# Paged decode attention inside a hybrid decoder layer: page order within a step, one list of cross-attention logit units, a tag for turned keys, and an earlier decay projection

## The chip, the cores and the metric

The kernel runs on one core of a Trainium2 chip (trn2). The metric is the device time of one execution in microseconds (us), lower is better. TensorE (PE in the profile) multiplies, VectorE (DVE), ScalarE (ACT) and GpSimd (POOL) work on vectors, SyncE (SP) issues nearly all DMA transfers, and each engine runs its own instructions strictly in the order in which they were written down for it.

## The reference, cut to what matters

One layer serves 512 prompt rows and 32 sample rows (8 sequences of 4 tokens) with the same weights; all arrays are float32.

```python
h = rmsnorm(x, norm_mix_g)
sq, sk, sv, gq, gk, gv, ga, gb, gz = split_cols(h @ w_in, IN_SPLITS)
o_sb  = stick_breaking_attention(q, k_all, v_all, ...)      # sample: 512 past tokens in 4 pages of 128, read through page_table
o_gdn = gated_delta_rule(...)                               # decay from ga, beta from gb
x = x + concat([o_sb, rmsnorm(o_gdn) * silu(gz)]) @ w_out
xq = rmsnorm((rmsnorm(x) @ w_xq).reshape(..., 4, 128))
attn = softmax(einsum('bshd,bmhd->bhsm', xq, mem_k) * 128 ** -0.5)   # sample: 256 cached memory tokens per sequence
x = x + einsum('bhsm,bmhd->bshd', attn, mem_v) @ w_xo
x = x + (silu(gate) * up) @ w_down
```

The change touches the sample side of the stick-breaking heads (`sb_sample`), the sample side of cross-attention (`cross_sample`), the decay of the gated-delta heads (`gates`), and the pacing of the gated-delta heads (`gdn_head`, `gdn_sample`, `invert`).

## The kernel before, in words

**Two kinds of work.** The dense work is projections: each float32 weight tile is split into a high and a low part (`wh`, `wl`) and each activation tile likewise (`ah`, `al`), and three products of 128x272 columns are accumulated for each half of the 544 rows (line 218; line 1598 for `w_xo`, line 2039 for gate and up, line 1919 for down). All else is side work, small matmuls with vector work between them: attention heads, the triangular inverses of the gated-delta heads, the sample rows.

**How the order is made.** Side work is written as Python generators. A `Side` object steps them from inside the dense loops (`side.tick` in `products`). Each `yield cost, latency` says how much PE time the step took and how long to leave that generator alone before its next step; the latency is counted in the dense and side time that was emitted meanwhile. A bigger latency puts more dense matmuls between a producer and its consumer. A scheduler then sets the final order of each engine's instructions. The feed-forward part (from about 1511 us on) is ordered by hand, and the change does not touch it.

**Stages.** Eight stick-breaking heads (to about 460 us), the decay columns (`gates`), eight gated-delta heads (to about 1050 us), the gates `gz`, `w_out` with the memory keys and values beside it, the `w_xq` projection, `w_xo` in two parts (columns 0 to 271, then 272 to 543; 16 blocks `m` of 12 matmuls each), then gate, up and down.

**`sb_sample`** runs twice, for heads 0 to 3 and 4 to 7. Its logits (`sample_logits`) go by units: a unit loads keys (`page`, 128x512), turns them with four transposes (line 968) into PSUM, ACT copies them to `kT` (line 699), and four matmuls at four column positions of the array multiply them with query windows `win` (line 711). Its values (`sample_values`) go by steps of four pages, one page for each of four sequences. Each page is one matmul of 128x512 at its own column position (line 752, `tile_position=(0, b * 32)`), so that four can run in the array at the same time. Six loads are kept ahead and seven buffers hold pages. A float32 matmul that is not a transpose is two instructions in the trace, so one page shows as x2 there and as x1 in the order.

**`cross_sample`** does the same for the 4 cross-attention heads: 16 units of keys (`xk`, line 1477), one pass over eight sequences for each of two pairs of heads, then a softmax (`xz`, `e`, from line 1487), then 16 value tiles (`xv`, line 1518), then a selection of the result (`selv`, line 1530). Its tiles come from the tags `ah` and `al` of the activation pool (16 buffers each) once the activations there are done: `c.tt` gives tag `ah`, `c.tp` gives tag `al`. It must be done before part 1 of `w_xo`: line 1585 drains the side work between the two parts.

```python
        if part:
            side.drain()
            pairs[-1].first()
```

**`gates`** (line 783) projects 16 columns of `w_in` for decay and beta, turns them, and makes the per-head factors; it is called once, after the eighth stick-breaking head was projected.

Of the kernel before, what the change touches and what calls it, by code (L numbers as in the profile page):

```python
# [15 lines left out]
P = 128  # L16
# [7 lines left out]
NB = 8  # L24
# [563 lines left out]
def sb_sample(c, g):  # L588
# [4 lines left out]
    for i, x in enumerate((q, k)):  # L593
        nc.vector.tensor_mul(sq[:, i * P : (i + 1) * P], x, x)
    yield 0.0, 2.0
    ps = c.aux()
# [34 lines left out]
    yield 0.3  # L631

    psz = c.aux()
    for h2 in range(2):

        def load(b, i):
            return load_pages(c, c.cache_k, [b * PAGES + i * 2 + j for j in range(2)], g * 4 + h2 * 2, 2)

        ps = yield from sample_logits(c, q, h2 * 2, load, 2)
        zt = c.tt("zt")  # L640
        nc.scalar.copy(zt[:, :256], ps[:, :256])
        yield 0.0, 1.0
# [32 lines left out]

def sample_logits(c, q, h0, load, n, ps=None, col=0):

    nc = c.nc
    w = c.tt("win")
    nc.gpsimd.memset(w[:, :512], 0.0)
    win = w[:, :512].rearrange("p (b h x) -> p b h x", b=NB, h=2)
    for b in range(NB):
        x = q[:, h0 * 32 : (h0 + 2) * 32].rearrange("p (h b t) -> p h b t", h=2, b=NB)[:, :, b]
        nc.gpsimd.tensor_copy(win[:, b, :, b * 4 : b * 4 + 4], x)
    yield 0.0, 3.0
    if ps is None:  # L690
        ps = c.aux()
    units = [(b, i) for b in range(NB) for i in range(n)]
    nxt = []

    def ahead():
        if units:
            pt = transposes(c, load(*units.pop(0)))
            k = c.tt("kT")
            nc.scalar.copy(k[:, :512], pt)
            nxt.append(k)  # L700

    ahead()
    yield 0.4, 0.2
    ahead()
    yield 0.4, 0.5
    for u in range(NB * n):
        b, i = divmod(u, n)
        k = nxt.pop(0)
        o = col + i * P
        for x in range(4):  # L710
            nc.tensor.matmul(
                ps[x * 32 : x * 32 + 32, o : o + P], win[:, b, x % 2, :], k[:, x * P : (x + 1) * P],
                start=u == 0 and col == 0, stop=b == NB - 1, skip_group_check=True, tile_position=(0, x * 32),
            )
        ahead()
        yield 0.7, 0.4
    return ps


def sample_values(c, w, n, load):  # L720
# [22 lines left out]
    for _ in range(6):  # L743
        ahead()
    yield 0.1, 1.5
    pso = c.aux()
    for half in range(2):
        ps = c.aux()
        for i in range(n):
            for b in range(4):  # L750
                x = ((i % 2) * NB + half * 4 + b) * 32
# [31 lines left out]
def gates(c, acts, rstd):  # L783
# [3 lines left out]
    ab = c.tt("ab")  # L787
    nc.vector.tensor_mul(halves(ab)[:16], ps[:16, :, :HT], halves(rstd)[:16])

    pt = c.aux()  # L790
# [109 lines left out]
def invert(c, gt, nc_, levels, res):  # L900
# [28 lines left out]
    for s in levels:  # L929
# [26 lines left out]
        nc.vector.tensor_sub(second[0], second[0], second[1])  # L956
        yield 0.22 * nc_, 1.1
        if s != levels[-1]:
# [80 lines left out]
def gdn_head(c, h, qkv):  # L1039
# [51 lines left out]
    for a in range(4):  # L1091
# [34 lines left out]
    nc.vector.tensor_mul(v3(on), v3(on), col(f, 4))  # L1126
    yield 0.0, 3.0
    ps = transposes(c, on)
# [16 lines left out]
def gdn_sample(c, g):  # L1145
# [294 lines left out]
def cross_sample(c, qs, outs, scale, tiles):  # L1440
# [13 lines left out]
    nc.vector.scalar_tensor_tensor(f, f, c.g_xq, r[:, :P], ALU.mult, ALU.mult)  # L1454
    yield 0.3, 2.5

# [10 lines left out]

    for h2 in range(2):
        if h2:
            some(0)  # L1470

        def load(b, i):
            if h2 or b >= 2:
                t = c.tt("xk")[:, :512]
            else:
                t = c.pb.tile([P, 4, P], F32, tag="wh", name="xk", bufs=XO_KEPT).rearrange("p k m -> p (k m)")
            nc.sync.dma_start(
                t.rearrange("p (a h d) -> p a h d", a=2, h=2), c.cache_mk[0, b, :, h2 * 2 : h2 * 2 + 2].rearrange("(a p) h d -> p a h d", p=P)
            )
            return t  # L1480

        ps = yield from sample_logits(c, f, h2 * 2, load, 1, ps if h2 else None, h2 * P)
    some(1)
# [753 lines left out]
def kern(ctx: ExitStack, tc: tile.TileContext, *args, stop=99):  # L2237
# [28 lines left out]
    with tc.tile_pool(name="pb", bufs=1) as pb:  # L2266
# [144 lines left out]
```

## Time and profile before

| what | us |
|---|---|
| median of 3 runs (2948.82 to 2950.75) | 2950.06 |
| the profiled execution | 2949.45 |
| its span, first to last instruction | 2947.8 |
| PE busy | 2864.5 |
| DVE busy | 2009.0 |
| ACT busy | 1447.9 |
| POOL busy | 721.7 |

The profile has a page for the whole execution and views for parts of it: sums in windows of time (with the granted TensorE clock, 1.00 being full speed, and the share of time that the 16 DMA engines were busy), a timeline of instructions with the idle time of the engine before each in brackets and what ended it, and a list of who waited for whom. Since matmuls are pipelined, a matmul's duration is not its cost: the cost is the distance from its start to the start of the next one.

### The profile page before, as it was taken

How to read it: one execution, taken by the hardware profiler on the slowest of the kernel's cores; microseconds unless marked ns; L12 is line 12 of the kernel's file. 1: busy time of each engine (PE TensorE's matmuls, PEld its weight loads, DVE VectorE, ACT ScalarE, POOL GpSimd, SP SyncE). 2: the span in 40 equal slices, each digit the busy share in tenths (PEclk: the TensorE clock that was granted, in tenths of full speed). 3: DMA queues.
4: the chain of work that ended last, by engine and by line, in shares of the span. 5: the costliest groups of instructions: out<-in, count | busy, mean ns of one | idle time of the engine just before them, and what ended most of it. 6: DMA issues, size and time to landing. Idle time of an engine off the chain costs nothing. (4 is left out here: it accounts for less than half of the span.)

```text
span 2947.8 us, 57119 instructions
## 1 busy us (share of the span) xinstructions
PE 2864.5 (97%) x22442; PEld 2725.5 (92%) x22442; DVE 2009.0 (68%) x3168; ACT 1447.9 (49%) x2760; POOL 721.7 (24%) x858
## 2 busy tenths in 40 slices
PE   8999999999999999999789999999999999999998
PEld 7997797788989999999679999999999999999998
DVE  5553344566686654437378888888888887888886
ACT  5455335443445354425555444444444446555675
POOL 3121111112212210003142343433333324211200
PEclk9999999999999999999899999999999999999999
DMA  7335534542343465532444554555455548966653
GB/s 224 94 95 151 173 97 132 166 125 70 97 132 86 119 214 152 151 114 83 151 140 120 169 169 150 162 161 161 149 163 169 150 135 259 272 199 199 189 172 96
DMA packets 632693, 442.72 MB, mean 150 GB/s; under 512 B 36107, under 2 KB 559704, under 8 KB 632424
## 3 DMA queue, kind: packets, MB, share of 16 engines
q1 hardware_dynamic: 600600, 384.64, 44.4%
q0 software_dynamic: 22176, 42.90, 4.7%
q10 hardware_dynamic: 9648, 11.54, 1.1%
q8 instruction: 176, 2.88, 0.4%
q14 instruction: 93, 0.76, 0.1%
HBM read 359.23 MB, written 79.75 MB: 149 GB/s over the span
## 5 line engine op out<-in xcount | busy, mean ns | idle before, releaser
L2039 PE MATMUL gu<-pr,wh 128*128 128x272 f32 x4944 | 674.4, 289 | 6.7 <-ACT pr L1668 3.0
L2039 PEld LDWEIGHTS gu<-pr,wh 128*128 128x128 f32 x4944 | 642.7, 189 | 8.4 <-ACT pr L1668 3.4
L218 PE MATMUL mm<-ah,wh 128*128 128x272 f32 (+1 forms) x2464 | 546.6, 301 | 6.0 <-ACT ah L334 3.7
L218 PE MATMUL mm<-al,wh 128*128 128x272 f32 (+1 forms) x2464 | 522.7, 291 | 0.7 <-DVE al L249 0.7
L218 PE MATMUL mm<-ah,wl 128*128 128x272 f32 (+1 forms) x2464 | 516.5, 290 | 0.1
L1919 PE MATMUL bank<-pr,wh 128*128 128x272 f32 x2464 | 466.6, 289 | 2.0 <-ACT bank L1947 1.3
L218 PEld LDWEIGHTS mm<-ah,wh 128*128 128x128 f32 (+1 forms) x2464 | 388.6, 188 | 37.9 <-issue 24.3
L207 DVE TENSOR_TENSOR wl<-wr,wh 128x512 fp32r<-128x512 f32 (+1 forms) x340 | 246.7, 729 | 233.0 <-ACT wh L206 227.0
L218 PEld LDWEIGHTS mm<-al,wh 128*128 128x128 f32 (+1 forms) x2464 | 388.8, 188 | 12.1 <-issue 9.1
L1919 PEld LDWEIGHTS bank<-pr,wh 128*128 128x128 f32 x2464 | 385.9, 188 | 4.1 <-ACT bank L1947 3.1
L218 PEld LDWEIGHTS mm<-ah,wl 128*128 128x128 f32 (+1 forms) x2464 | 386.1, 188 | 2.6 <-issue 1.0
L206 ACT CAST wh<-wr 128x512 fp32r<-128x512 f32 (+1 forms) x340 | 208.0, 614 | 325.4 <-PE mm L218 268.5
L2039 PE MATMUL gu<-pr,wl 128*128 128x272 f32 x2472 | 361.7, 289 | 2.0 <-DVE wl L1817 2.0
L1919 PE MATMUL bank<-pr,wl 128*128 128x272 f32 x1232 | 354.5, 288 | 0.0
L2039 PEld LDWEIGHTS gu<-pr,wl 128*128 128x128 f32 x2472 | 330.1, 189 | 2.4 <-issue 2.0
L1817 DVE TENSOR_TENSOR wl<-sum,wh 128x1024 fp32r<-128x1024 f32 x172 | 221.0, 1285 | 75.3 <-ACT wh L1813 75.3
L1919 PEld LDWEIGHTS bank<-pr,wl 128*128 128x128 f32 x1232 | 232.0, 188 | 0.0
L1813 ACT CAST wh<-sum 128x1024 fp32r<-128x1024 f32 x172 | 180.5, 1050 | 77.5 <-PE gu L2039 46.7
L1817 DVE TENSOR_TENSOR wl<-raw,wh 128x1024 fp32r<-128x1024 f32 x133 | 202.6, 1524 | 15.7 <-ACT wh L1813 13.7
L1813 ACT CAST wh<-raw 128x1024 fp32r<-128x1024 f32 x133 | 140.0, 1053 | 102.4 <-PE gu L2039 93.0
L2104 POOL DMA_DIRECT2D pr<-hT x154 | 82.1, 547 | 254.5 <-PE bank L1919 227.6
L1806 DVE TENSOR_TENSOR sum<-raw,sum 128x1024 f32<-128x1024 f32 x86 | 135.6, 1577 | 1.0
(530 smaller groups left out, 4173.2 us busy)
## 6 DMA issues: line engine op xcount, KB each, us to landing
raw<-in_w_gate_up SPq DMA_DIRECT2D x176, 512.0 KB
wr<-in_w_in SPq DMA_DIRECT2D x108, 512.0 KB
raw<-in_w_down SPq DMA_DIRECT2D x176, 256.0 KB
hT<-hs SPq DMA_DIRECT2D x154, 272.0 KB
pr<-hT POOLq DMA_DIRECT2D x154, 272.0 KB, 6.7
page<-in_cache_sb_k SPq DMA_DIRECT2D x128, 128.0 KB
page<-in_cache_sb_v SPq DMA_DIRECT2D x64, 256.0 KB
wr<-in_w_out SPq DMA_DIRECT2D x32, 512.0 KB
```

The source lines that it names most:

```text
L206: nc.scalar.copy(hi[:, :m, :n], raw[:, k : k + m, :n])
L207: nc.vector.tensor_sub(lo[:, :m, :n], raw[:, k : k + m, :n], hi[:, :m, :n].bitcast(F32))
L218: c.nc.tensor.matmul(ps[:n, h, :HT], l[:, :n], r[:, h * HT : (h + 1) * HT], start=first and i == 0, stop=last and i == 2,)
L1806: self.f.c.nc.vector.tensor_sub(self.a[q], self.a[x], self.a[y])
L1813: self.f.c.nc.scalar.copy(self.hi[q], self.left(q))
L1817: self.f.c.nc.vector.tensor_sub(self.lo[q], self.left(q), self.hi[q].bitcast(F32))
L1919: self.c.nc.tensor.matmul(self.c.bank[bank][:, o], t[x][:, s, i * P : (i + 1) * P], pairs[i].op[q][r], start=new and not (i or n), stop=se ...
L2039: self.c.nc.tensor.matmul(bank, w[:, i * P : (i + 1) * P], self.pairs[i].op[q][r], start=start and n == 0, stop=n == 23, skip_group_check= ...
L2104: self.c.nc.gpsimd.dma_start(t, self.hT[2 * g + pair, :, max(0, 2 * n - 1) + k])
```

## The change

Five edits, all in the order and pacing of the sample side work; no arithmetic is added or taken away.

1. **Values.** In a step of four pages, the matmul of the page that was loaded last (index 3) is emitted first, then 0, 1, 2, in `sample_values` and in `cross_sample`. The latency after a step of `sample_values` becomes 8.0 (from 1.0), after the first loads 5.0 (from 1.5), after a selection 3.0 (from 0.5).
2. **Logits.** `sample_logits` takes a list of units. The query windows are made ahead of it by `query_windows`, for both pairs of heads at once. In `cross_sample` all 16 units are one list, so the two-unit start of the pipeline occurs once instead of twice. The cost of a unit is stated as 0.6 (from 0.7).
3. **Turned keys.** `kT` comes from `c.tp`, seen as float32. In `cross_sample` this moves it from tag `ah` to tag `al`; in `sb_sample` both are the same tag.
4. **Decay.** `gates` becomes a generator: its projection is emitted ahead of the projections of the eighth stick-breaking head, the rest of it where it was.
5. **Latencies.** Larger ones in `sb_sample`, `invert`, `gdn_head` and `gdn_sample`.

```diff
@@ sb_sample
-    yield 0.0, 2.0
+    yield 0.0, 3.5
...
+    wins = [query_windows(c, q, h2 * 2) for h2 in range(2)]
+    yield 0.0, 5.0
     psz = c.aux()
     for h2 in range(2):
-        def load(b, i):
-            return load_pages(c, c.cache_k, [b * PAGES + i * 2 + j for j in range(2)], g * 4 + h2 * 2, 2)
-
-        ps = yield from sample_logits(c, q, h2 * 2, load, 2)
+        def load(b, i, h0=g * 4 + h2 * 2):
+            return lambda: load_pages(c, c.cache_k, [b * PAGES + i * 2 + j for j in range(2)], h0, 2)
+
+        ps = yield from sample_logits(c, [(wins[h2][b], i, load(b, i), b == NB - 1) for b in range(NB) for i in range(2)])
@@ 
-def sample_logits(c, q, h0, load, n, ps=None, col=0):
+def query_windows(c, q, h0):
     nc = c.nc
     w = c.tt("win")
...
-    yield 0.0, 3.0
-    if ps is None:
-        ps = c.aux()
-    units = [(b, i) for b in range(NB) for i in range(n)]
-    nxt = []
+    return [win[:, b] for b in range(NB)]
+
+
+def sample_logits(c, units):
+    nc = c.nc
+    ps = c.aux()
+    todo, nxt = list(units), []
 
     def ahead():
-        if units:
-            pt = transposes(c, load(*units.pop(0)))
-            k = c.tt("kT")
-            nc.scalar.copy(k[:, :512], pt)
+        if todo:
+            pt = transposes(c, todo.pop(0)[2]())
+            k = c.tp("kT")[:, :512].bitcast(F32)
+            nc.scalar.copy(k, pt)
             nxt.append(k)
...
-        yield 0.7, 0.4
+        yield 0.6, 0.4
@@ sample_values
-    yield 0.1, 1.5
+    yield 0.1, 5.0
...
-            for b in range(4):
+            for b in (3, 0, 1, 2):
...
-            yield 0.9, 1.0
+            yield 0.9, 8.0 if i < n - 1 else 1.0
...
-        yield 0.5, 0.5
+        yield 0.5, 3.0
@@ gates, behind the projection
     nc.vector.tensor_mul(halves(ab)[:16], ps[:16, :, :HT], halves(rstd)[:16])
+    yield
@@ invert, behind the second product of a level
-        yield 0.22 * nc_, 1.1
+        yield 0.22 * nc_, 1.7
@@ gdn_head
-        yield 0.22, 1
+        yield 0.22, 1.6
...
-    yield 0.0, 3.0
+    yield 0.0, 4.5
@@ gdn_sample, behind silu
-    yield 0.0, 4.0
+    yield 0.0, 6.5
@@ cross_sample
-    yield 0.3, 2.5
+    wins = [query_windows(c, f, h2 * 2) for h2 in range(2)]
+    yield 0.3, 5.0
...
-    for h2 in range(2):
-        if h2:
+    def load(b, h2):
+        if h2 == 1 and b == 0:
             some(0)
...
-        ps = yield from sample_logits(c, f, h2 * 2, load, 1, ps if h2 else None, h2 * P)
+    ps = yield from sample_logits(c, [(wins[h2][b], h2, lambda b=b, h2=h2: load(b, h2), b == NB - 1) for h2 in range(2) for b in range(NB)])
...
-            for b4 in range(4):
+            for b4 in (3, 0, 1, 2):
@@ kern
         for h in range(8):
             settle(h)
+            if h == 7:
+                decay = gates(c, acts, rstd)
+                next(decay)
...
-        gates(c, acts, rstd)
+        next(decay, None)
```

Three places of PE's order show what the edits move. In the rows, `page,win` is one page's value matmul, `kT,win` a unit's logit matmuls, `ident,xk` a unit's transposes, `mm` a dense projection.

Values of the first `sb_sample`, PE, before (a stretch of the second and third step):

```order
L752 MATMUL aux<-page,win 32x512
L218 MATMUL mm<-ah,wh 128x272 x2
L218 MATMUL mm<-al,wh 128x272 x2
L218 MATMUL mm<-ah,wl 128x272 x2
L752 MATMUL aux<-page,win 32x512
L218 MATMUL mm<-ah,wh 128x272 x2
L218 MATMUL mm<-al,wh 128x272 x2
L218 MATMUL mm<-ah,wl 128x272 x2
L752 MATMUL aux<-page,win 32x512 x2
```

The same place after the change:

```order
L218 MATMUL mm<-al,wh 128x272 x2
L218 MATMUL mm<-ah,wl 128x272 x2
L757 MATMUL aux<-page,win 32x512 x4
L218 MATMUL mm<-ah,wh 128x272 x2
L218 MATMUL mm<-al,wh 128x272 x2
L218 MATMUL mm<-ah,wl 128x272 x2
L533 MATMUL aux<-hat,raw 128x128
```

Before, a step's pages stand one or two at a time between dense matmuls; after, the four stand together. Over both calls of `sb_sample` the 64 value matmuls stand in 37 rows before (one of them holds seven, from the end of one step and the next) and in 20 rows after, 12 of four and 8 of two.

The end of the first part of `w_xo`, PE, before (the last row is the first of part 1):

```order
L968 MATMUL aux<-ident,xk 128x128 x4
L711 MATMUL aux<-kT,win 32x128 x4
L968 MATMUL aux<-ident,xk 128x128 x4
L711 MATMUL aux<-kT,win 32x128 x4
L1493 MATMUL aux<-xz,ident 64x128 x4
L968 MATMUL aux<-ident,e 128x128 x2
L1518 MATMUL aux<-xv,win 32x512 x8
L1530 MATMUL aux<-selv,os 128x16 x4
L1518 MATMUL aux<-xv,win 32x512 x8
L1530 MATMUL aux<-selv,os 128x16 x4
L1598 MATMUL mm<-xh,wh 128x272 x2
```

After the change, the value matmuls of cross-attention stand among the matmuls of part 0:

```order
L1523 MATMUL aux<-xv,win 32x512 x8
L1603 MATMUL mm<-xh,wh 128x272
L1603 MATMUL mm<-xl,wh 128x272
L1603 MATMUL mm<-xh,wl 128x272
L1603 MATMUL mm<-xh,wh 128x272
L1603 MATMUL mm<-xl,wh 128x272
L1603 MATMUL mm<-xh,wl 128x272
L1535 MATMUL aux<-selv,os 128x16 x4
L1523 MATMUL aux<-xv,win 32x512 x4
L1603 MATMUL mm<-xh,wh 128x272
L1603 MATMUL mm<-xl,wh 128x272
L1603 MATMUL mm<-xh,wl 128x272
```

Before, the last four units, the softmax and all values stand in one piece behind the last dense matmul of part 0; after, the last selection stands a block `m` ahead of the end of part 0, and no side work is left between the parts. On the way there, six units of `xk` and `kT` stand almost side by side, with one to three dense matmuls here and there.

The recurrence of a gated-delta head, PE, before (`ve,TT` makes what DVE scales into the operand of `ve,kn`):

```order
L1105 MATMUL aux<-ve,TT 128x128
L218 MATMUL mm<-ah,wl 128x272
L218 MATMUL mm<-ah,wh 128x272 x2
L218 MATMUL mm<-al,wh 128x272 x2
L218 MATMUL mm<-ah,wl 128x272 x2
L218 MATMUL mm<-ah,wh 128x272 x2
L1110 MATMUL aux<-ve,kn 128x128
```

The same step of the same head after:

```order
L1111 MATMUL aux<-ve,TT 128x128
L218 MATMUL mm<-ah,wh 128x272
L218 MATMUL mm<-al,wh 128x272 x2
L218 MATMUL mm<-ah,wl 128x272 x2
L218 MATMUL mm<-ah,wh 128x272 x2
L218 MATMUL mm<-al,wh 128x272 x2
L218 MATMUL mm<-ah,wl 128x272 x2
L218 MATMUL mm<-ah,wh 128x272 x2
L218 MATMUL mm<-al,wh 128x272 x2
L218 MATMUL mm<-ah,wl 128x272 x2
L1116 MATMUL aux<-ve,kn 128x128
```

Nine dense matmuls stood between the two, now seventeen. On SP, the first four of the loads of `xk` that wait for freed activation buffers stand ahead of the eighth load of `w_xo` instead of behind it, and the last five loads of `w_xo` stand behind the `xk` loads and most of the `xv` loads.

More of the change, by code (lines that the diff above doesn't have):

```diff
@@ L705, in sample_logits @@
     yield 0.4, 0.5
-    for u in range(NB * n):
-        b, i = divmod(u, n)
+    for u, (win, column, _, last) in enumerate(units):
         k = nxt.pop(0)
-        o = col + i * P
+        o = column * P
         for x in range(4):
             nc.tensor.matmul(
-                ps[x * 32 : x * 32 + 32, o : o + P], win[:, b, x % 2, :], k[:, x * P : (x + 1) * P],
-                start=u == 0 and col == 0, stop=b == NB - 1, skip_group_check=True, tile_position=(0, x * 32),
+                ps[x * 32 : x * 32 + 32, o : o + P], win[:, x % 2, :], k[:, x * P : (x + 1) * P],
+                start=u == 0, stop=last, skip_group_check=True, tile_position=(0, x * 32),
             )
         ahead()
-        yield 0.7, 0.4
+        yield 0.6, 0.4
     return ps
@@ L1466, in some @@
         values.append([loadv(i // 2 * 4 + b, i % 2) for b in range(4)])
-    for h2 in range(2):
-        if h2:
+    def load(b, h2):
+        if h2 == 1 and b == 0:
             some(0)
[L1472 to L1480, printed above, removed]
-        ps = yield from sample_logits(c, f, h2 * 2, load, 1, ps if h2 else None, h2 * P)
+        if h2 or b >= 2:
+            t = c.tt("xk")[:, :512]
+        else:
+            t = c.pb.tile([P, 4, P], F32, tag="wh", name="xk", bufs=XO_KEPT).rearrange("p k m -> p (k m)")
+        nc.sync.dma_start(
+            t.rearrange("p (a h d) -> p a h d", a=2, h=2), c.cache_mk[0, b, :, h2 * 2 : h2 * 2 + 2].rearrange("(a p) h d -> p a h d", p=P)
+        )
+        return t
+    ps = yield from sample_logits(c, [(wins[h2][b], h2, lambda b=b, h2=h2: load(b, h2), b == NB - 1) for h2 in range(2) for b in range(NB)])
     some(1)
```

## The prediction, as it was put on record before the changed kernel was run

> **What bounds the kernel now.** I read the page first, then the sums in windows, then TensorE's timeline in the two places where the windows differ from the rest, then the waits.
>
> ```profile
> PE 2864.5 (97%) x22442; PEld 2725.5 (92%) x22442; DVE 2009.0 (68%) x3168; ACT 1447.9 (49%) x2760; POOL 721.7 (24%) x858
> ...
> 1400.00:1500.00 100.00, 80.36 (x619) 63.93 (x618) 41.91 (x97) 52.37 (x130) 24.51 (x42) 0.86 0.45 140
> ...
> 1600.00:1700.00 100.00, 100.00 (x799) 100.00 (x798) 86.11 (x85) 46.31 (x61) 32.84 (x20) 1.00 0.52 156
> ```
>
> In the windows the columns are PE, weight load, DVE, ACT and POOL busy, the granted clock, the DMA share and GB/s. TensorE is the bound: it idles 2947.8 - 2864.5 = 83 us in all, and in a dense stretch it starts 799 matmuls in 100 us, 0.125 us each. So an edit here can gain in two ways only: it ends idle time of TensorE, or it shortens side work that takes TensorE from the dense matmuls. The stretch 1400 to 1500 stands out, with 619 matmuls and a clock of 0.86. It is cross-attention. Split at the end of part 0 of `w_xo` and at the start and end of part 1, and with TensorE's timeline from there, it shows why:
>
> ```profile
> 1404.00:1455.00 51.00, 45.19 (x373) 38.62 (x372) 25.32 (x58) 31.19 (x80) 11.45 (x28) 0.93 0.48 150
> 1455.00:1487.00 32.00, 18.18 (x114) 8.52 (x113) 5.35 (x17) 11.73 (x33) 4.87 (x7) 0.68 0.41 124
> 1487.00:1512.00 25.00, 24.90 (x194) 24.20 (x193) 21.65 (x45) 15.87 (x29) 13.01 (x10) 1.00 0.73 223
> ```
>
> ```profile
> 1455.30 0.28 PE L1598 MATMUL mm<-xh,wl 128*128 128x272 f32 x1
> 1457.12 0.63 PE L968 MATMUL aux<-ident,xk 128*128 128x128 f32 x4 [1.54 <-DMA xk<-in_cache_mem_k]
> 1458.58 0.63 PE L711 MATMUL aux<-kT,win 128*32 128x128 f32 x8 [0.82 <-ACT kT L699]
> 1461.18 1.08 PE L968 MATMUL aux<-ident,xk 128*128 128x128 f32 x4 [1.98 <-DMA xk<-in_cache_mem_k]
> ...
> 1473.13 0.66 PE L968 MATMUL aux<-ident,e 128*128 128x128 f32 x2 [2.13 <-DVE e L1396]
> 1475.45 3.64 PE L1518 MATMUL aux<-xv,win 128*32 128x512 f32 x16 [1.65 <-POOL acc L270]
> ...
> 1484.85 1.06 PE L1530 MATMUL aux<-selv,os 128*128 128x16 f32 x8 [0.68 <-ACT os L1526]
> 1486.61 0.52 PE L1598 MATMUL mm<-xh,wh 128*128 128x272 f32 x2 [0.70 <-ACT xh L1537]
> ```
>
> From 1455.4 to 1486.6 no dense matmul runs: four units, the softmax and the values go one after the other, each waiting for a load or another engine, at a clock of 0.68.
>
> **The values of `sb_sample`: 18 us.** In the timeline of the first call, x8 is four pages, x2 one, x4 two:
>
> ```profile
> 330.56 1.06 PE L752 MATMUL aux<-page,win 128*32 128x512 f32 x8 [0.40 <-POOL win L731]
> 331.56 0.52 PE L218 MATMUL mm<-ah,wh 128*128 128x272 f32 x2
> ...
> 334.59 1.04 PE L752 MATMUL aux<-page,win 128*32 128x512 f32 x2
> 335.56 0.52 PE L218 MATMUL mm<-ah,wh 128*128 128x272 f32 x2
> ...
> 336.52 1.05 PE L752 MATMUL aux<-page,win 128*32 128x512 f32 x4
> 337.50 0.52 PE L218 MATMUL mm<-ah,wh 128*128 128x272 f32 x2
> ```
>
> Start to next start, four pages take 331.56 - 330.56 = 1.00, one page 0.97, two 0.98. A group costs the same however many of the four column positions it fills. The order shows 37 rows of such matmuls before, of which the one with seven pages must be two groups, so 38, and 20 after. 18 x 0.98 = 17.6 us leave TensorE's path. The groups lie between dense matmuls with hardly an idle moment, so I take all of it: 18, from 14 (some groups still stretched by a late page) to 19.
>
> One rule speaks against so much. The Trainium skill ("TensorE: Matmul & The Clock Gate", Part 3, measured speedup) puts four packed row tiles at 3.07 times a single one, not four; by that estimate a full step would cost 0.98 x 4 / 3.07 = 1.28, the 12 full ones 12 x 0.3 = 3.6 more, and the gain would be 14. The row with x8 above, 1.00, says otherwise for columns, and the measurement decides.
>
> What the new order adds is a wait in front: the first matmul of a step now needs the last load, and behind it on TensorE stand the dense matmuls, that is everything. The loads keep six ahead of need, so a step's last two are issued when the step before it frees its pages:
>
> ```profile
> 331.64 16.03 SPq L777 DMA_DIRECT2D page<-in_cache_sb_v  x16
> ...
> PE aux L752 <- DMA page<-in_cache_sb_v: 0.2, 1, 0.2
> ```
>
> Before, 16 pages were issued in 16 us and TensorE waited for pages 0.2 us in all, so DMA gives a page per microsecond. The new latency of 8.0 sets the steps some 8 us of emitted work apart, four pages each. I cost the wait at nothing; the cover is that spacing, and without it the price is in the rivals.
>
> **Cross-attention: 16.5 us.** In the order after the change nothing stands between the parts, so the piece from 1455.42 to 1486.61, 31.2 us, goes, and its work moves among the matmuls of part 0. That work is not free. What a unit costs there is seen in the units that already lie there:
>
> ```profile
> 1443.16 0.29 PE L1598 MATMUL mm<-xh,wh 128*128 128x272 f32 x1
> 1443.29 0.60 PE L968 MATMUL aux<-ident,xk 128*128 128x128 f32 x4
> ...
> 1443.85 0.29 PE L1598 MATMUL mm<-xh,wl 128*128 128x272 f32 x1
> ...
> 1444.61 0.29 PE L1598 MATMUL mm<-xh,wl 128*128 128x272 f32 x1
> 1444.88 0.42 PE L711 MATMUL aux<-kT,win 128*32 128x128 f32 x8
> ...
> 1445.47 0.29 PE L1598 MATMUL mm<-xl,wh 128*128 128x272 f32 x1
> ```
>
> Two dense matmuls and the transposes take 1443.85 - 1443.16 = 0.69, so the transposes 0.44; likewise 0.86 - 0.25 = 0.61 for the logits. Four units are 4.2. `xz` is as narrow as a unit's logits, 0.6; the two transposes of `e` 0.2; 16 value matmuls in four groups at 0.98, 3.9; the selections at most their 1.06 each at the slow clock, say 1.8 together. Sum 10.7; 31.2 - 10.7 = 20.5 gained.
>
> Three things change that. First, in the 51 us of part 0 and the heads before it TensorE idles 5.8 already (51.00 - 45.19). Some of that goes, because `kT` no longer takes turns with `xk` in one tag and the first `xk` loads no longer queue behind a load of `w_xo` on SP: 3 gained (0 to 5.8). Second, six units now stand almost side by side, each `kT` needing ACT's copy of the unit just turned; the tail above shows 0.8 for that wait, so 4 lost (0 to 8, the upper end with a stretch of half clock). ACT on average has room: 31.19 + 11.73 = 43 us in the 62 that the stage would take. Third, the tail was a rest for DVE, 5.35 of 32.00, while in part 1 behind it DVE has 21.65 of 25.00. What it caught up there now falls into part 1 and the start of gate and up: 3 lost (0 to 6). The loads of `w_xo` that moved behind `xv` I cost at nothing: the cover is that six blocks of part 1 keep their weights, 6 x 12 x 0.125 = 9 us in which the next can land. Together 20.5 + 3 - 4 - 3 = 16.5, from 8 to 26.
>
> **The latencies and the decay: 8 us.** The waits of TensorE between 190 and 1060 us at whose producers a `yield` grew, or a step moved:
>
> ```profile
> PE aux L1110 <- DVE ve L1106: 4.7, 5, 2.8
> PE aux L913 <- DVE TT L956: 3.1, 3, 1.6
> PE aux L1166 <- POOL sqk L859: 2.7, 2, 1.5
> PE aux L968 <- DVE on L1126: 2.1, 3, 1.3
> PE aux L597 <- DVE sq L594: 2.0, 2, 1.0
> PE aux L792 <- DVE ab L788: 1.7, 1, 1.7
> PE aux L711 <- POOL win L688: 1.5, 1, 1.5
> ```
>
> They sum to 17.8. The order shows eight dense matmuls more, 1.0 us, between `ve,TT` and `ve,kn`, which covers most such waits but not the longest, 2.8, where DVE was late for its own reasons. Where one wait goes the next is somewhat late. I take a little under half, 8, from 0 to 18. The decay projection moves with its two narrow weight loads ahead of the eighth head's loads; the same matmuls run, and its wait of 1.7 is in the sum. The windows made at once are two memsets and 16 small copies on POOL, 24% busy, earlier by one pass; that is in the 1.5.
>
> A wait can also cost clock, and here trace and rule part:
>
> ```profile
> 766.00 2.74 PE L1206 MATMUL aux<-sqk,s 128*128 128x8 f32 x24
> ...
> 769.00:776.00 7.00, 7.00 (x36) 7.00 (x34) 0.54 (x2) 1.11 (x2) 1.02 (x1) 0.51 0.45 131
> ```
>
> Behind 24 matmuls of eight columns the clock is 0.51 for 7 us, with TensorE busy all the time. That costs up to 3.5 us, and the order after has a longer run of these, 20 matmuls or x40 in the trace, so I expect it again and count no gain. The Trainium skill (same page, "HAM oscillation") gives the rule as no idle gap over some 3.4 us; by it neither this stretch nor the tail, whose longest wait is 2.13, should have slowed, and the clock could neither give nor take here. The trace disagrees in both places; the sum stays 8, with 3.5 either way inside its bounds.
>
> **Sum.** 18 + 16.5 + 8 = 42.5. From the profiled execution, 2949.45 (1.65 outside its span, 0.6 below the median of the runs), this gives 2907.
>
> **The rivals.** *Cross-attention gives it back:* part 0 becomes a chain of copies and waits, and DVE's backlog lands on gate and up. For it: DVE's 21.65 of 25.00; against: ACT's 43 in 62. Then cross-attention brings 4 and the sum is 30: 2919. *Everything goes:* part 0 swallows all without a wait, and three quarters of the waits in the heads go: 19 + 26 + 14 = 59, 2890. *The last page blocks:* if each of the 16 steps waits for its last page, the whole core waits. The point from which it decides is (42.5 + 5.9) / 16 = 3.0 us a step; at 4 us the time is 2949.45 - 42.5 + 64 = 2971, slower. For it: four pages are 1 MB, and SP issues them in line with weight loads that may block; against: the 0.2 above. *It doesn't do what it says:* the groups close up, but TensorE then idles for weights as long, and the stage of cross-attention is held by its loads: within 6 us of 2949.
>
> **How the numbers follow.** Forecast 0.60 (its own range 2894 to 2917), given back 0.18, everything 0.15, last page 0.04, no change 0.03. The bound of what counts as a change is 0.2%, 5.9 us. The bounds of the terms add up to 22 (14 + 8 + 0) and 63 (19 + 26 + 18), which is 2927 and 2886; this range takes in the first three cases and leaves out the ends of the last two. Faster 0.93, same 0.03, slower 0.04.
>
> **What would show it.** Right: `page,win` in the timeline as x8 at about 1.00; no stretch without dense matmuls between the two parts of `w_xo`, part 1 starting some 45 us earlier than 1486.6 (18 from the values, 8 from the heads, 19.5 from part 0); the waits for `ve` and `TT` at about half. Wrong: a wait for `page` of microseconds before each step; `kT` or `xk` waits in part 0 summing to over 10 us; long waits for `pr` or `wl` at the start of gate and up; or the sum of the waits in the heads unchanged under new names.

## The result and the profile after

The changed kernel takes 2918.34 us (median of four runs, 2914.71 to 2921.17) where the kernel before takes 2949.44 beside it: a ratio of 0.9898, 95% interval 0.9880 to 0.9915, or 30 us less. The forecast was 2907, the range 2886 to 2927. The profiled execution is 2919.49, 30.0 below that of before, and it is read here. First the page's row of TensorE, after the change:

```profile
PE 2844.4 (97%) x22442; PEld 2726.1 (93%) x22442; DVE 2006.2 (69%) x3168; ACT 1447.2 (50%) x2760; POOL 718.9 (25%) x858
```

TensorE is busy for 20 us less with the same 22442 matmuls, so most of the gain is matmul time and not idle time. Where it lies is found by taking the same dense matmul in both traces, since their number and sequence are the same. The 5377th, at the end of the attention heads, starts at 1077.1 before and 1069.7 after: 7.4 gained. The first of part 1 of `w_xo` starts at 1486.6 and 1458.6: 28.0 gained. The end is 30.0 earlier. So what lies between the two, cross-attention above all, brought 20.6 and the heads 7.4, where the prediction had 16.5 and 26.

The timeline of TensorE in the first `sb_sample` after the change has the value matmuls as forecast:

```profile
326.83 1.07 PE L757 MATMUL aux<-page,win 128*32 128x512 f32 x8
327.83 0.52 PE L218 MATMUL mm<-ah,wh 128*128 128x272 f32 x2
...
337.22 1.07 PE L757 MATMUL aux<-page,win 128*32 128x512 f32 x8
338.21 0.52 PE L218 MATMUL mm<-ah,wh 128*128 128x272 f32 x2
```

Four pages stand together and take 1.00 and 0.99, start to next start, without a wait in front. The sums in windows for part 0 of `w_xo` with all of cross-attention, and for the start of part 1, and below them TensorE's timeline at the seam:

```profile
1396.00:1458.60 62.60, 56.15 (x485) 44.90 (x483) 29.72 (x72) 42.10 (x110) 15.59 (x34) 0.97 0.54 177
1458.60:1486.00 27.40, 27.26 (x196) 26.41 (x197) 22.79 (x48) 16.65 (x33) 13.99 (x12) 0.94 0.73 225
```

```profile
1444.06 1.92 PE L1523 MATMUL aux<-xv,win 128*32 128x512 f32 x16
...
1446.78 1.05 PE L1535 MATMUL aux<-selv,os 128*128 128x16 f32 x8
...
1447.75 1.07 PE L1523 MATMUL aux<-xv,win 128*32 128x512 f32 x8
...
1453.65 1.06 PE L1535 MATMUL aux<-selv,os 128*128 128x16 f32 x8
...
1458.60 0.52 PE L1603 MATMUL mm<-xh,wh 128*128 128x272 f32 x2 [2.29 <-ACT xh L1542]
```

The 31 us without dense matmuls are gone; what is left of the seam is one wait of 2.29. Part 0 is at a clock of 0.97, and ACT's 42.10 in 62.60 left room for the copies of `kT`.

The heads are where the forecast failed. The waits of TensorE between 190 and 1060 us after the change (total, times, longest):

```profile
PE aux L960 <- DVE X L956: 6.2, 2, 4.5
PE aux L715 <- POOL win L686: 4.1, 2, 2.8
PE aux L919 <- DVE TT L962: 3.9, 2, 3.3
PE aux L1111 <- DVE ve L1108: 3.1, 3, 1.3
PE aux L974 <- POOL cv L865: 2.3, 3, 1.0
PE aux L715 <- ACT kT L704: 1.8, 2, 1.3
```

These are the longest; all rows of this view add up to 30.5, against 24.3 before. The waits for `ab` (1.7) and for `ve` at `ve,kn` (4.7, now 1.1) went as forecast, and longer ones came for `X`, `win` and `TT` (`X` and `TT` are tiles of the triangular inverses).

To follow this through the experiments I split the time up to the 5377th dense matmul into three accounts. *Waits* is the idle time ahead of matmuls, counted above 0.1 us. *Clock* is half of the time in which TensorE was busy at half clock, an upper estimate: in the changed kernel two dense matmuls take 0.45 there, start to next start (754.87 to 755.32), and 0.25 at full clock. *Work* is the rest. The count starts at the first dense matmul, which is 0.3 earlier after the change, so that the heads show 7.1 here and not 7.4. Differences against the kernel before, in us, each from one profiled execution:

| kernel | work | waits | clock | heads in all |
|---|---|---|---|---|
| changed | -21.5 | +5.8 | +8.6 | -7.1 |
| values alone | -24.1 | +8.9 | +6.5 | -8.8 |
| latencies of the heads alone | -5.4 | 0.0 | -3.4 | -8.8 |
| changed, head latencies as before | -23.3 | +4.9 | -0.4 | -18.7 |
| changed, late convolution | -25.2 | +2.1 | +2.5 | -20.6 |
| changed, scalings on DVE | -20.5 | -0.7 | +3.4 | -17.8 |
| page order alone | -25.4 | +10.6 | +6.8 | -8.0 |
| pace of the values alone | -25.0 | +8.5 | +4.1 | -12.4 |
| changed, `kT` in its old tag | -21.9 | +5.7 | +11.9 | -4.3 |
| changed, two lists | -22.1 | +6.1 | +11.6 | -4.4 |
| head latencies as before, late convolution | -21.9 | -1.5 | -1.7 | -25.1 |
| head latencies as before, scalings on DVE | -23.2 | -3.3 | -2.0 | -28.6 |

The work fell by more than the 18 that the forecast gave it. Waits and clock took 14 of it back. The rows for `kT` in its old tag and for two lists show how far one execution is to be trusted: up to there both kernels have the same order on TensorE as the changed one, and their clock differs from its by 3.

### The profile page after: what moved, and what is told of

It is laid out like the page before. It is cut to its first block, busy times and chain, and to the rows that moved or that the text cites. A ratio compares the mean times of both kernels' runs of the same rounds, so it can differ in the third digit from the quotient of the medians.

```text
span 2917.8 us, 57065 instructions
## 1 busy us (share of the span) xinstructions
PE 2844.4 (97%) x22442; PEld 2726.1 (93%) x22442; DVE 2006.2 (69%) x3168; ACT 1447.2 (50%) x2760; POOL 718.9 (25%) x858
## 5 line engine op out<-in xcount | busy, mean ns | idle before, releaser
L218 PEld LDWEIGHTS mm<-ah,wh 128*128 128x128 f32 (+1 forms) x2464 | 389.7, 189 | 33.7 <-issue 20.5
L1822 DVE TENSOR_TENSOR wl<-raw,wh 128x1024 fp32r<-128x1024 f32 x133 | 202.9, 1527 | 15.3 <-ACT wh L1818 13.4
```

The lines of the kernel that those rows point to most:

```text
L218: c.nc.tensor.matmul(ps[:n, h, :HT], l[:, :n], r[:, h * HT : (h + 1) * HT], start=first and i == 0, stop=last and i == 2,)
L1822: self.f.c.nc.vector.tensor_sub(self.lo[q], self.left(q), self.hi[q].bitcast(F32))
```

## The experiments

Three theories were tried. *One:* the larger latencies cost by themselves, since waits move on to the next consumer. *Two:* the slower pace of the values pushes `sb_sample` and `gdn_sample` to other places beside the gated-delta heads, and that costs. *Three*, formed after the first four runs: POOL's convolution of the sample rows holds up one operation that DVE needs, and DVE, in order, holds up TensorE. Each kernel was timed against the kernel before on its own chip, and times are compared by these ratios: a ratio times 2949.44 stands for us.

**The parts alone.** First the values:

```diff
-    yield 0.1, 1.5
+    yield 0.1, 5.0
-            for b in range(4):
+            for b in (3, 0, 1, 2):
-            yield 0.9, 1.0
+            yield 0.9, 8.0 if i < n - 1 else 1.0
-        yield 0.5, 0.5
+        yield 0.5, 3.0
```

> The kernel before with the page order (3, 0, 1, 2) and the three latencies of the values alone. Both theories expect groups of four pages as x8 at 1.00 us and 17.5 us less of TensorE's time for the values. Theory one (the larger latencies of the heads cost by themselves, the values are innocent) expects nearly all of it as time: 2949.4 - 17.5 = 2932, from 2929 to 2936, and waits of the heads as before. Theory two (the slower pace of the values pushes them into the gated-delta heads, and that displacement costs) expects the loss of about 10 to be here: 2942, from 2938 to 2948, with more groups of the state update ex,kns and more half clock.

Ratio 0.9960 (0.9946 to 0.9973), 12 us less. Its waits between 560 and 1060 us begin so:

```profile
PE aux L954 <- DVE X L950: 7.3, 3, 4.6
PE aux L940 <- DVE X L936: 4.1, 1, 4.1
```

The page matmuls cost 20.4 less, but the waits for `X` of the changed kernel are here too, without any larger latency in the heads. That speaks for theory two. Then cross-attention, with the windows made ahead and the page order of its values:

```diff
-            k = c.tt("kT")
-            nc.scalar.copy(k[:, :512], pt)
+            k = c.tp("kT")[:, :512].bitcast(F32)
+            nc.scalar.copy(k, pt)
...
-    for h2 in range(2):
...
+    ps = yield from sample_logits(c, [(wins[h2][b], h2, lambda b=b, h2=h2: load(b, h2), b == NB - 1) for h2 in range(2) for b in range(NB)])
```

> The kernel before with the edits of cross-attention alone: one list of units, windows ahead, kT in the other tag, the page order of its values. Both theories expect what the stage gained in the full change, 20 us: 2929, from 2926 to 2933. If the stage gains only because the heads before it end otherwise, it is less than 12: over 2937.

Ratio 0.9907 (0.9891 to 0.9922), 27 us less, more than the 20 expected; by the profiled executions 22.9, of which 0.7 lie in the heads, where TensorE's order is that of the kernel before. Behind the heads it gains 22.2, the changed kernel 22.5, so this part does not depend on the others. Then the larger latencies:

```diff
-    yield 0.0, 2.0
+    yield 0.0, 3.5
...
-        yield 0.22 * nc_, 1.1
+        yield 0.22 * nc_, 1.7
...
-        yield 0.22, 1
+        yield 0.22, 1.6
...
-    yield 0.0, 3.0
+    yield 0.0, 4.5
...
-    yield 0.0, 4.0
+    yield 0.0, 6.5
```

> The kernel before with the five larger latencies of the heads alone (sb_sample 3.5, invert 1.7, gdn_head 1.6 and 4.5, gdn_sample 6.5), the decay where it was. Theory one expects slower by about 8: 2957, from 2952 to 2963, with ve,kn waits of TensorE down by about 3 and waits for TT up by more. Theory two expects the gain that the prediction gave them, 8 less: 2941, from 2936 to 2946.

Ratio 0.9975 (0.9962 to 0.9987), 7 us less: theory one falls in this form. But its waits between 190 and 1060 us show that the prediction's reason was wrong as well:

```profile
PE aux L1105 <- DVE ve L1102: 5.5, 6, 1.6
PE aux L940 <- DVE X L936: 4.0, 1, 4.0
```

All rows add up to 24.9, against 24.3 before. The wait of 2.8 at `ve,kn` is gone and others stand one consumer on. What fell is work, by 5.4, and the cost of half clock, by 3.4. Of the work about 3 is page groups that closed, 34 rows of `page,win` in place of 37, which the prediction's values term counts already. And the reverse, the changed kernel with four of the latencies as before:

```diff
-        yield 0.22 * nc_, 1.7
+        yield 0.22 * nc_, 1.1
...
-        yield 0.22, 1.6
+        yield 0.22, 1
...
-    yield 0.0, 4.5
+    yield 0.0, 3.0
...
-    yield 0.0, 6.5
+    yield 0.0, 4.0
```

> The changed kernel with the latencies of invert, gdn_head and gdn_sample as before (1.1, 1, 3.0, 4.0); page order, pace of the values, cross-attention, decay and the 3.5 of sb_sample as changed. Theory one expects the loss to go: 2918.3 - 9 = 2909, from 2905 to 2914. Theory two expects the small gain of the latencies to go and the loss to stay: 2924, from 2919 to 2928.

Ratio 0.9870 (0.9855 to 0.9885), 38 us less, so 8 better than the changed kernel (0.9898), though the ends of the two intervals overlap. The same latencies bring 7 alone and cost about 8 beside the other edits. Each result fits one theory, this one the first and the one before the second; neither foresaw both. The three parts alone bring 12 + 27 + 7 = 46 by the ratios, each with an interval of some 4 us either way, near the prediction's 42.5; together they bring 30. By the profiled executions it is 39 against 30. The rest of the change (the windows made at once in `sb_sample`, the stated cost of a unit there, the earlier decay) was run in no kernel by itself, so its share of the difference is not known.

**What the latencies do in company.** The account says clock: 15.4 us lost to half clock in the heads of the changed kernel, 6.4 with the old latencies, a difference three times the 3 us between executions of one order. Beside it `ex,kns`, the update of the sample states, costs 3.9 of work more than in the kernel before. TensorE's timeline of the changed kernel, and the sums over the stretch around it:

```profile
747.72 0.96 PE L1212 MATMUL aux<-sqk,s 128*128 128x8 f32 x8
748.53 1.14 PE L955 MATMUL aux<-T,gt 128*128 128x128 f32 x8
749.50 5.14 PE L1212 MATMUL aux<-sqk,s 128*128 128x8 f32 x40
```

```profile
743.70:760.10 16.40, 16.40 (x117) 16.30 (x116) 5.57 (x15) 5.72 (x13) 1.31 (x2) 0.79 0.34 100
```

With the old latencies the same matmuls stand in groups of eight records among dense matmuls:

```profile
749.22 0.95 PE L1212 MATMUL aux<-sqk,s 128*128 128x8 f32 x8
750.03 0.49 PE L218 MATMUL mm<-ah,wh 128*128 128x272 f32 x2
...
750.86 0.95 PE L1212 MATMUL aux<-sqk,s 128*128 128x8 f32 x8
```

```profile
741.00:761.00 20.00, 20.00 (x170) 19.50 (x168) 7.90 (x14) 5.40 (x10) 1.31 (x2) 1.00 0.60 173
```

TensorE is busy throughout both stretches; only the mixture differs, and the clock is 0.79 in the one and 1.00 in the other. The prediction knew of this longer run of narrow matmuls in the order and counted it at no change. The matmuls of `ex,kns`, each on 32 rows of the array, are written in pairs that run side by side:

```profile
804.15 1.99 PE L1265 MATMUL aux<-ex,kns 32*128 32x512 f32 x8
806.07 0.52 PE L218 MATMUL mm<-ah,wh 128*128 128x272 f32 x2
...
813.15 1.12 PE L1265 MATMUL aux<-ex,kns 32*128 32x512 f32 x2
814.20 0.52 PE L218 MATMUL mm<-ah,wh 128*128 128x272 f32 x2
```

Two pairs take 1.92, and one matmul that lost its partner takes 1.05, as much as a pair. The order has them in 7 rows before, 10 after, 7 again with the old latencies. It is what the change mended for the pages, undone for another group. That the order of these groups decides the clock is argued from the two stretches; no run changed it alone.

**Pace or page order.** The two halves of the values' edit, each alone on the kernel before:

```diff
-            for b in range(4):
+            for b in (3, 0, 1, 2):
```

> The kernel before with the page order (3, 0, 1, 2) alone, the latencies of the values as they were (1.5, 1.0, 0.5). In the order it has 16 rows of page,win, so the groups close without the latencies. If the slower pace of the values is what brings the extra waits and half clock of the values-alone kernel, this one keeps the whole 17 to 20 us: 2949.4 - 18 = 2931, waits of the heads near the 29 us of before. If any shift of the work brings them, it lands with the values-alone kernel, about 12 below the kernel before: 2938. And a step of four pages behind a short latency may now wait for its last page, at 1 us per page up to 2 us for each of 16 steps.

Ratio 0.9945 (0.9929 to 0.9961), 16 us less. The groups close (21.4 less for `page,win`), and the wait comes that the prediction had left to the pace; its first row of waits:

```profile
PE aux L752 <- DMA page<-in_cache_sb_v: 10.5, 12, 2.4
```

The other half:

```diff
-    yield 0.1, 1.5
+    yield 0.1, 5.0
-            yield 0.9, 1.0
+            yield 0.9, 8.0 if i < n - 1 else 1.0
-        yield 0.5, 0.5
+        yield 0.5, 3.0
```

> The kernel before with the three latencies of the values alone (5.0, 8.0, 3.0), pages in the old order. In the order it has 17 rows of page,win, as few as with the page order. If the pace is what closes the groups and what shifts the heads, it equals the values-alone kernel, about 12 below the kernel before: 2938. If the page order is needed as well, groups of one and two pages show in the timeline and the gain is under 6.

Ratio 0.9958 (0.9941 to 0.9974), 12 us less, and `page,win` 20.4 less. So the pace closes the groups by itself, the page order does so too, and neither adds to the other. The pace pays with waits for `X` (4.7 and 4.1 the longest), the order with waits for pages. So theory two holds for the waits for `X`, but not for the loss as a whole: the heads gain 8.0 with the order alone, without any slower pace, and 8.8 with both.

**What holds X.** In the changed kernel TensorE waits 4.54 for `X` at 708.73:

```profile
708.73 1.98 PE L960 MATMUL aux<-TT,X 128*128 128x128 f32 x8 [4.54 <-DVE X L956]
```

DVE's timeline ahead of it, and below it POOL's, where L1163 and L1165 are the convolution of the sample rows in `gdn_sample`:

```profile
699.91 0.90 DVE L1073 SCALAR_TENSOR_TENSOR cumrow<-cumrow,neg 128x512 f32<-128x512 f32 x1
706.27 0.69 DVE L1083 TENSOR_TENSOR gt<-gt,aux 128x512 f32<-128x512 f32 x1 [5.45 <-POOL gt L1082]
707.38 0.69 DVE L1088 TENSOR_TENSOR cumrow<-cumrow,aux 128x512 f32<-128x512 f32 x1 [0.43 <-POOL cumrow L1087]
707.99 0.68 DVE L956 TENSOR_TENSOR X<-aux,lev 128x512 f32<-128x512 f32 x1
```

```profile
695.55 0.42 POOL L1163 TENSOR_TENSOR sqk<-raws,convw 128x128 f32<-128x128 f32 x1
...
704.78 0.45 POOL L1165 TENSOR_TENSOR sqk<-sqk,sctmp 128x128 f32<-128x128 f32 x1
705.19 1.04 POOL L1082 TENSOR_TENSOR gt<-cumrow,sm 128x512 f32<-128x512 f32 x1
```

POOL works through the convolution from 695.55 to 705.19, with one other operation in between, and only then scales `gt`. DVE stands for 5.45 before it, and `X`, two places behind on DVE, is made at 707.99, though TensorE had its product ready by 702.3. POOL is 25% busy on average, and here it is the bound. The same pattern stands at 953 with `TT`. It stood in the kernel before too, with the convolution on POOL from 723.62 on: DVE waited 3.57 for `gt`, and TensorE 2.79 for `ve` of the head ahead:

```profile
734.60 0.69 DVE L1077 TENSOR_TENSOR gt<-gt,aux 128x512 f32<-128x512 f32 x1 [3.57 <-POOL gt L1076]
736.72 0.49 PE L1110 MATMUL aux<-ve,kn 128*128 128x128 f32 x2 [2.79 <-DVE ve L1106]
```

So the change did not create the collision, it moved it to a costlier place. Two kernels take the collision away, in different ways.

```diff
 def gdn_sample(c, g):
     nc = c.nc
+    yield 0.0, 16.0
     qk_ = c.tt("sqk")
```

> The changed kernel with a latency of 16.0 as the first step of gdn_sample, so that POOL's convolution of the sample rows (18 steps, 15 us) stands behind the scaling of gt of the same head on POOL and not ahead of it. Theory three (POOL's convolution holds gt, gt holds DVE, and DVE's late X and TT hold TensorE, which then runs at half clock) expects the waits of 4.5 us for X near 709 and 3.3 us for TT near 953 to go, and half of the half clock with them: 2918.3 - 12 = 2906, from 2902 to 2911. If the late X and TT come from the larger latencies and not from POOL, it stays within 4 of 2918.

Ratio 0.9834 (0.9818 to 0.9850), 49 us less, so 19 better than the changed kernel, where theory three expected 12. Both waits are gone. A new one of 4.5 stands at 958: DVE waits 3.71 for POOL's `g` (L891), which now stands amid the second call's convolution.

```diff
-    nc.gpsimd.tensor_mul(v3(gt), v3(dec), col(br2, 4))
+    nc.vector.tensor_mul(v3(gt), v3(dec), col(br2, 4))
...
-    nc.gpsimd.tensor_mul(v3(dec), v3(dec), col(rk, 4))
+    nc.vector.tensor_mul(v3(dec), v3(dec), col(rk, 4))
```

> The changed kernel with the two scalings of gt and dec in gdn_head moved from POOL to DVE (16 more operations of 128x512 on DVE, 0.69 us each, 11 us in all). Theory three expects the same two waits to go, less what 11 us more on DVE cost the split of the weights: 2909, from 2904 to 2915. If POOL is not the cause, DVE's added work makes it slower: 2920 or more.

Ratio 0.9850 (0.9832 to 0.9869), 44 us less, 14 better than the changed kernel, and this with 16 operations more on DVE, which is busy for 16.5 us longer. DVE's timeline at the same place:

```profile
698.41 0.69 DVE L1082 TENSOR_TENSOR gt<-cumrow,sm 128x512 f32<-128x512 f32 x1 [0.76 <-ACT cumrow L1076]
699.21 0.69 DVE L1083 TENSOR_TENSOR gt<-gt,aux 128x512 f32<-128x512 f32 x1
699.82 0.68 DVE L1087 TENSOR_TENSOR cumrow<-cumrow,sm 128x512 f32<-128x512 f32 x1
700.42 0.68 DVE L956 TENSOR_TENSOR X<-aux,lev 128x512 f32<-128x512 f32 x1
```

`X` is made at 700.42 instead of 707.99, and the waits of TensorE around it no longer list it. This edit leaves TensorE's order as it was up to that place, but for a few neighbours that swap, and waits fall by 6.5 in the account; of the 5.2 by which clock falls some 3 can be spread. For the two longest waits of the heads theory three is shown.

**Which part of the cross edit.** The changed kernel with `kT` back in its old tag:

```diff
-            k = c.tp("kT")[:, :512].bitcast(F32)
+            k = c.tt("kT")[:, :512]
```

> The changed kernel with kT of sample_logits back in tag ah; one list, windows and everything else as changed. If the tag is what brings the gain of cross-attention, the tail between the parts of w_xo comes back in the order (two units, softmax and all values behind the last dense matmul of part 0) and most of the 20 us with it: 2918.3 + 17 = 2935, from 2930 to 2941. If the single list or the freed loads bring it, it stays within 5 of 2918.

Ratio 0.9970 (0.9959 to 0.9981), 9 us less than the kernel before: 21 of the 30 are lost. Behind the heads its profiled execution gains nothing, 0.9 later than before where the changed kernel gains 22.5. Its timeline at the end of part 0 reads like that of the kernel before:

```profile
1457.61 0.63 PE L974 MATMUL aux<-ident,xk 128*128 128x128 f32 x4 [1.45 <-DMA xk<-in_cache_mem_k]
...
1462.08 1.08 PE L974 MATMUL aux<-ident,xk 128*128 128x128 f32 x4 [2.42 <-DMA xk<-in_cache_mem_k]
...
1483.33 0.82 PE L1603 MATMUL mm<-xh,wh 128*128 128x272 f32 x2 [1.67 <-ACT xh L1542]
```

And the changed kernel with two lists:

```diff
-    ps = yield from sample_logits(c, [... for h2 in range(2) for b in range(NB)])
+    ps = None
+    for h2 in range(2):
+        ps = yield from sample_logits(c, [... for b in range(NB)], ps)
```

> The changed kernel with the 16 units of cross-attention as two lists of eight again, so that the pipeline of units starts twice; kT in the new tag. If the tag brings the gain, this loses only the second start, 0 to 5: 2920, from 2916 to 2924. If the single list brings it: 2930 or more.

Ratio 0.9910 (0.9895 to 0.9925), 27 us less. Behind the heads its profiled execution gains 18.8 where the changed kernel's gains 22.5. So the tag brings nearly all of the gain of cross-attention. In the trace it is TensorE's waits for `xk` that come and go with it, 1.45 and 2.42. SP shows where the loads stand, first with the old tag, then in the changed kernel:

```profile
1453.19 0.37 SPq L1578 DMA_DIRECT2D wr<-in_w_xo  x1
1453.65 0.47 SPq L1482 DMA_DIRECT2D xk<-in_cache_mem_k  x1
1457.44 0.37 SPq L1578 DMA_DIRECT2D wr<-in_w_xo  x1
1457.90 0.46 SPq L1482 DMA_DIRECT2D xk<-in_cache_mem_k  x1
```

```profile
1409.94 15.52 SPq L1482 DMA_DIRECT2D xk<-in_cache_mem_k  x7
```

With the old tag the last five loads of `xk` come one at a time, some 4.2 us apart, each behind a load of `w_xo`; in the changed kernel the last seven come in a row and are out by 1425.46. SP's waits ahead of the loads of `xk` themselves are no longer with the old tag (10.7 us between 1380 and 1500 us against 13.4), so the loads are late by their place behind those of `w_xo`. That the tag gives them this place because the turned keys of earlier units hold their buffers is argued from the code. The single list is worth at most the 4 that are left, and the intervals overlap.

**Both mended at once.** The old head latencies with either cure of the collision; the edits are those shown above.

> The changed kernel with the latencies of invert, gdn_head and gdn_sample as before and the latency of 16.0 ahead of POOL's convolution. If the larger latencies cost 8 to 10 and POOL's convolution 12 to 18, each by itself, the sum is 2918.3 - 8 - 15 = 2895. If both are the same loss (either edit moves the convolution away from gt), it equals the changed kernel with the late convolution alone, about 18 below the changed kernel: 2900. More than 2908 would say that the two spoil each other.

> The changed kernel with the latencies of invert, gdn_head and gdn_sample as before and the two scalings of gt and dec on DVE. Same question as with the late convolution: 2918.3 - 8 - 13 = 2897 if the two losses add, 2905 if they are one.

Ratios 0.9847 (0.9834 to 0.9861) and 0.9827 (0.9811 to 0.9843), 45 and 51 us less: 2904 and 2898 where the changed kernel's ratio stands for 2919. With the late convolution the old latencies add nothing that the ratios show (0.9834 with the larger ones), so there the two losses look like one. With the scalings on DVE the sum of 2897 comes out, but 0.9850 with the larger latencies overlaps with 0.9827, so by the ratios that stays open. The account of the heads has the old latencies ahead both times, by 4.5 and 10.8, of which some 3 can be spread. The last kernel beats both the kernel before and the changed one.

## Why the prediction was partly wrong, by its own steps

**The values, 18 off TensorE's path: right.** All `page,win` matmuls cost TensorE 37.3 before and 19.8 after, start to next start: 17.5. The cover named for the wait for the last page was the pace, and the kernel with the page order alone shows what it covers: 10.5 us in 12 waits, 0.9 each where the rival needed 3.0. The doubt from the Trainium skill ("TensorE: Matmul & The Clock Gate", Part 3) would by that estimate have made a full step 1.28 and the gain 14; four pages took 1.00 again.

**Cross-attention, 16.5: right, 4 too little.** The tail went as counted. The two losses that were set against it hardly came. For the six units side by side 4 was taken; apart from one wait of 2.69 for the first `kT`, which stands in the kernel before as well, `kT` and `xk` cost 0.4. For DVE's backlog 3 was taken; from the first dense matmul of part 1 to the first after another 288 it is 40.8 before and 41.0 after. The rival that gives it back is refuted, and with the first of the prediction's signs: part 0 has no chain of waits. Its 2919 is the nearest of the forecasts to the measured time by coincidence, since the loss came in the heads. By its own bounds this term should have gone down to 20.5 - 8 - 6 = 6.5, not 8.

**The latencies, 8: this step failed.** The prediction took "a little under half" of 17.8 us of waits as gain, on the ground that eight more dense matmuls cover them. In the changed kernel the waits of the heads rose by 5.8 and half clock cost 8.6 more. With the old latencies it is 4.9 and -0.4, so the larger latencies took no waits away, neither there nor alone (0.0), and what they cost in company is half clock, 9.0. The step treated each wait as a distance between a producer and a consumer on TensorE. The longest were held by a third engine, POOL, with DVE in order behind it, and there a longer distance only changes which consumer is caught. The row that gave it away was in the list, 4.7 us for `ve` with one of 2.8, "where DVE was late for its own reasons"; asking what DVE waited for would have found `gt` and the convolution. That the latencies alone do bring 7 does not save the step, since their waits sum to 24.9, as good as the 24.3 of before, and 3 of the 7 are page groups: the number came out by luck.

**The sum.** The terms were added as if each left the places of the rest alone. Alone they bring about what was said, 46 by the ratios and 39 by the profiled executions; together they bring 16 or 9 less. That the time still lies in the range is partly luck: the heads gained 7.4 where the lower bounds of values and latencies add up to 14, and the room that cross-attention left unused made up for it. The sign named for it came, the waits of the heads under new names, and part 1 of `w_xo` starts 28.0 earlier instead of 45.

**Small terms.** Making the windows at once was put inside an existing wait of 1.5; it is 4.1 now, since at 479.71 the first logits wait 2.76 with sixteen copies of windows on POOL ahead of them instead of eight. The earlier decay removed its wait of 1.7; it was not run alone. Half clock was given 3.5 either way, and the change moved it by 8.6.

## What to carry to other kernels

When TensorE waits for a vector engine, follow the wait to that engine's own queue before adding distance: an engine that is 25% busy on average can be the bound for 10 us, and then taking two operations off it, or putting its other work later, ends a wait that more distance only moved. Pacing edits that share one stream of work need not add up; make each alone, and then look at what each does to the places of the others' groups. And where loads and intermediate results take buffers from one tag, giving them separate tags can be nearly the whole of a gain that a larger restructuring seems to bring.

## What the runs showed of the hardware

Half clock comes in stretches of 3.4, 6.8 or more us, multiples of 3.4 but for the one that the end of the program cuts off, and it follows idle time less closely than expected. In the changed kernel one starts beside a wait of 4.54 (at 708.9), another amid 40 records of narrow matmuls with TensorE busy (753.2, in the stretch shown above). Two more rows, from the sums in windows:

```profile
814.60:821.40 6.80, 6.80 (x24) 5.04 (x24) 3.88 (x15) 0.62 (x1) 0.00 (x0) 0.51 0.91 249
708.80:712.30 3.50, 3.50 (x17) 3.11 (x17) 0.89 (x2) 0.00 (x0) 2.48 (x6) 0.51 0.14 16
```

The first stands behind `ex,kns` matmuls without partners, which use 32 rows of the array, with TensorE busy throughout; the second is the one beside the wait of 4.54. The Trainium skill ("TensorE: Matmul & The Clock Gate", "HAM oscillation") speaks of an idle gap of some 3.4 us; the trace shows 3.4 as the length of the slow stretch, and slow stretches with no gap at all.

It is also not the same in each execution. The kernel with two lists has the same order on TensorE as the changed kernel up to the end of the heads, and the same waits there (35.3 and 35.0 in the account), but 41.0 us at half clock against 30.7, and the heads end 3.0 later. The kernel with `kT` in its old tag has that order too, and 41.0 as well. The stretches stand at the same six places in all three; what differs is their length, by one step of 3.4 at five of them. In the clock records of each execution all stretches begin on one grid of 3.41: in the changed kernel at 480.17, 708.86 and 753.23, which is 67 and 13 steps apart, and with two lists at 479.18 and 707.88, the grid 1.0 earlier against the same work. So where the work falls on that grid is a candidate for the difference; it was not tested. What decides a stretch was not isolated: no run changed the mixture of wide and narrow matmuls alone.
